# New operation costs, and explicit waits for carries and paired buffers, in the planner that orders a gated-DeltaNet layer's instructions

## The chip, the core and the metric

The kernel runs on one core of one Trainium2 chip. The metric is the device time of one execution in microseconds (us), from launch to end. The engines are named as in the profile: PE is TensorE (PEld is its weight loads), DVE is VectorE, ACT is ScalarE, POOL is GpSimd, and SP is SyncE, on whose queue all DMAs of this kernel are issued.

## What is computed

One layer over 2048 positions of width 1024, in fp32. RMSNorm, then one input projection to 7,184 columns, which feeds two branches; their outputs are joined and projected back by `w_out`, added to the residual, and a gated per-layer embedding and a last RMSNorm follow.

- Branch A, in 8 groups: `gelu(u) * (W_s LN(gelu(v)) + b) * silu(z)` over blocks of 128 positions.
- Branch B, in 8 heads of 128: a causal convolution of four taps over q, k and v, SiLU, L2-normed q and k, and the chunked delta rule in chunks of 64:

```
A = strict_lower((k*beta) k^T * L);  T = inverse(A + I)
u = T (v*beta);  w = T (k*beta*exp(decay));  qk = (q k^T) * L
per chunk:  v_new = u - w S;  o = q_dec S + qk v_new;  S = a S + k_dec^T v_new
```

## The kernel before

**Tiling.** The positions go in two passes of 1024. A product of fp32 matrices with 512 columns is made of three matmuls in a reduced fp32 format (`mm3`: high x high, high x low, low x high), the operands being split into a high and a low part by ACT (copy) and DVE (subtract). Each pass has four units for the branch A input v (`v_unit`), then for each of the 8 heads three units: `kq_unit` (k and q), `vu_unit` (v of branch B, u of branch A) and `zz_unit` (both gates). A unit is four projections of 24 matmuls of 512 columns, so a head has 288 of them. The output projection (`out_stream`) and the gate part (`gate_stream`) come last.

**Work of a head beside the projections.** `conv` (L573) takes a projection out of PSUM with two ACT copies, runs three multiply-adds on DVE, writes the last three columns to `carry` for the next block of 512 positions, and applies SiLU. `decay` (L671) makes the decay matrix L: two selections on POOL (`asel`, tiles R), two matmuls `pd` on PE, an exponential on ACT, one more selection on POOL. `front` (L699), twice a head, transposes k, splits k and q into high and low (`kqhi`, `kqlo`, in the same two buffers R), multiplies them (`pkq`), and scales the results into AT and QK on DVE; AT is stored to DRAM (`atd`, L761). After the second front, `inverse` (L791) loads A back in another layout (`ain`, L802) and inverts all 16 chunk matrices of the head on POOL: 63 steps of a multiplication (`xtmp`) and a subtraction (`xs`), both by `gtt` at L162. The result goes out to DRAM (`td`, L821) and comes back as `Dt` (L828). `chain` (L831) then walks the 8 blocks of 128 positions, five dependent steps each, PE and DVE or ACT in turn; its matmuls are `pc` and `po`. `finish` normalises the head's output (POOL `sso`), and `mix` does branch A.

**What sets the order.** Each engine runs its instructions in the order in which this Python program emits them, and waits on semaphores for operands and buffers. The order comes from a planner, class `Flow` (L36). It has a clock `t`, which each matmul pushes forward by its assumed cost, and a clock for DVE, ACT and POOL, which each operation pushes forward (`op`, L46). The helpers `mm`, `tr`, `act`, `tt`, `stt`, `ts`, `gtt`, `asel` and the like (L114 to L167) hold these costs in ns. `mm` returns the due time of its result, 170 ns after its assumed end; `op` returns the assumed end plus 110 ns. A projection is the stream (`drive`, L85); between any two of its matmuls, every side task whose due time has come goes on and emits what is next, PE work too. `room` (L55) holds a task until an engine's clock is at most 300 ns ahead; `take` and `give` count buffers. So a result that is due sooner in the plan than on the chip is awaited by PE, in order, with all that stands behind it. Two DMA round trips are in the plan as constants: 2500 and 4500 from the front to the first inversion step, 2600 and 4500 from the last step to the chain.

Of the kernel before, what the change touches and what calls it, by code (L numbers as in the profile page):

```python
# [15 lines left out]
F32R = mybir.dt.float32r  # L16
# [14 lines left out]
class Flow:  # L31
# [11 lines left out]
        self.count = 0  # L43
        self.used = {}

    def op(self, eng, cost, after=None):  # L46
        start = max(self.clk[eng], self.t if after is None else after)
        self.clk[eng] = start + cost
        return start + cost + 110.0

    def spawn(self, gen, delay=0.0, prio=0):
        self.tasks.append([prio, self.count, self.t + delay, gen])
# [1 line left out]

    def room(self, eng, slack=300.0):  # L55
        while self.clk[eng] > self.t + slack:
            yield self.clk[eng] - slack

    def free(self, tag):
        return lambda: self.used.get(tag, 0) < CAPS[tag]  # L60

    def take(self, tag):
        while self.used.get(tag, 0) >= CAPS[tag]:
            yield self.t + 150.0
        self.used[tag] = self.used.get(tag, 0) + 1

    def give(self, tag):
        self.used[tag] -= 1
# [32 lines left out]
def trunk(tc, a, out):  # L101
# [7 lines left out]
    fl = Flow()  # L109
# [4 lines left out]
    def mm(o, lhsT, rhs, start, stop):  # L114
        nc.tensor.matmul(o, lhsT, rhs, start=start, stop=stop)  # L115
        n = width(rhs)
        fl.t += max(107.0, 0.4216 * n) if lhsT.dtype == F32R else max(231.0, 1.68 * n)
        return fl.t + 170

    def tr(o, i, ident):  # L120
        nc.tensor.transpose(o, i, ident)
        fl.t += 109.0
        return fl.t + 170

    def act(o, i, func, after=None, **kw):
        nc.scalar.activation(o, i, func, **kw)  # L126
        c = 150 + 0.68 * width(i) + (90 if "accum_out" in kw else 0) + (60 if "scale" in kw else 0)
        t = TABLES.get(func)
        if t and t != fl.table:
            fl.table = t  # L130
            c += 1283
        return fl.op("act", c, after)

    def tt(o, x, y, op, after=None):
        nc.vector.tensor_tensor(o, x, y, op)  # L135
        return fl.op("dve", 69 + 1.04 * width(o), after)

    def stt(o, x, sc, y, op0, op1, after=None):
        nc.vector.scalar_tensor_tensor(o, x, sc, y, op0, op1)  # L139
        return fl.op("dve", 130 + 1.04 * width(o), after)  # L140

    def ts(o, x, s1, s2, op0, op1=None, after=None):
        if op1 is None:
            nc.vector.tensor_scalar(o, x, s1, s2, op0)
        else:
            nc.vector.tensor_scalar(o, x, s1, s2, op0, op1)  # L146
        return fl.op("dve", 70 + 1.0 * width(o), after)

    def vcopy(o, x, after=None):
        nc.vector.tensor_copy(o, x)  # L150
        return fl.op("dve", 65 + 1.04 * width(o), after)

    def recip(o, x, after=None):
        nc.vector.reciprocal(o, x)
        return fl.op("dve", 70 + 6.3 * width(o), after)

    def power(o, x, y, after=None):
        nc.gpsimd.tensor_tensor(o, x, y, ALU.pow)  # L158
        return fl.op("pool", 150 + 190 * width(o), after)

    def gtt(o, x, y, op, after=None):
        nc.gpsimd.tensor_tensor(o, x, y, op)  # L162
        return fl.op("pool", 250 + 1.88 * width(o), after)

    def asel(o, x, after=None):
        nc.gpsimd.affine_select(o, x, [[0, 4], [1, P]], ALU.is_ge, 0.0, 0, -1)  # L166
        return fl.op("pool", 570, after)  # L167

    with ExitStack() as outer:
        outer.enter_context(tc.manual_schedule())  # L170
# [399 lines left out]
            fl.give("uz")  # L570
            gz.append(us[b])

        def conv(ps, f, dest, ready):  # L573
            yield from fl.take("pre")
            yield from fl.take("acc")
            yield from fl.room("act")
            pre = gt("pre", "pre", [P, 515], 2)
            acc = gt("acc", "acc", [P, 512], 3)
            act(pre[:, 3:515], ps, AF.Copy)
            vcopy(pre[:, 0:3], carry[:, f, :])  # L580
            yield fl.clk["act"] - 300
            t = act(acc, ps, AF.Copy, scale=cw[:, f, 3:4])
            fl.give("pj")
            yield t
            for j in (2, 1, 0):
                yield from fl.room("dve")
                t = stt(acc, pre[:, j:j + 512], cw[:, f, j:j + 1], acc, ALU.mult, ALU.add)
            vcopy(carry[:, f, :], pre[:, 512:515])
            fl.give("pre")
            yield t  # L590
            yield from fl.room("act")
            if dest is None:
                t = act(acc, acc, AF.Silu)
            else:
                t = act(dest, acc.rearrange("p (u t) -> p u t", u=4), AF.Silu)
                fl.give("acc")
            yield t
            ready.append(acc)
# [8 lines left out]
        def vu_unit(X, p, ui, h, st):  # L607
            fetch(ui + 1)
            for b in range(2):
                ps = yield from proj(X, ui, 0, b)  # L610
                fl.spawn(conv(ps, 16 + h, None, st["V"]), 170, 1)
                if b == 0:
                    next_w(ui + 1, 0)
            yield lambda: len(mixed) == p * NH + h
            for b in range(2):
                ps = yield from proj(X, ui, 1, b, rest_w(ui + 1) if b == 1 else None)
                fl.spawn(u_post(ps, st["U"]), 170, 1)
# [29 lines left out]
        def kq_unit(X, p, ui, h, st):  # L647
            fetch(ui + 1)
            for b in range(2 if h else 0):
                fl.spawn(decay(p, h, b, st["i"]), 0, 2)  # L650
            for b in range(2):
                yield fl.free("kq")
                fl.used["kq"] = fl.used.get("kq", 0) + 1
                kq = gt("kq", "kq", [P, 4, 2, P], 4)
                ps = yield from proj(X, ui, 0, b)
                fl.spawn(conv(ps, 8 + h, kq[:, :, 0, :], st["C"][b]), 170, 1)
                ps = yield from proj(X, ui, 1, b, rest_w(ui + 1) if b == 1 else None)
                fl.spawn(conv(ps, h, kq[:, :, 1, :], st["C"][b]), 170, 1)
                st["KQ"].append(kq)
                fl.spawn(front(p, h, b, st), 3000, 1)  # L660
                if b == 0:
                    next_w(ui + 1, 0)
# [8 lines left out]
        def decay(p, h, b, i):  # L671
# [3 lines left out]
            while len(fronts) < i + b - 1 or len(Ls) < i + b:  # L675
                yield fl.t + 300
            R = []
            for gg in (gh, gl):
                yield from fl.take("R")
                yield from fl.room("pool", 800)  # L680
                r = gt("R", "R", [P, 4, P], 2, F32R)
                f = asel(r, gg[:, cs, None].bitcast(F32).to_broadcast([P, 4, P]))
                R.append(r)
# [15 lines left out]
        def front(p, h, b, st):  # L699
# [29 lines left out]
            for u2 in range(2):  # L729
                while len(st["C"][b]) < 2:  # L730
                    yield fl.t + 300
                yield from fl.take("R")
                yield from fl.take("R")
                hi = gt("R", "kqhi", [P, 2, 2, P], 2, F32R)
                lo = gt("R", "kqlo", [P, 2, 2, P], 2, F32R)
                yield from split_to(hi, lo, kq[:, u2 * 2:u2 * 2 + 2])
# [495 lines left out]

        done, fronts, inverted, SC, mixed, stored, vdone, prepped, Ls = [[] for _ in range(9)]
        xready = [0, 0]
        xs0 = x_load(0)
        ones = cp.tile([P, P], F32, name="ones")
        nc.vector.memset(ones, 1.0)
# [109 lines left out]
```

## Time and profile before

| | |
|---|---|
| median of 3 runs | 2353.34 us (2353.13 to 2359.31) |
| the profiled execution, its own time | 2353.73 us |
| its span, first to last instruction | 2352.0 us, 34,693 instructions |
| mean granted TensorE clock | 0.987 of 2.4 GHz |
| PE busy | 2269.4 us (96%) |
| DVE, ACT, POOL busy | 1312.9, 1013.6, 1113.1 us |
| ACT table loads | 116 of 1.283 us |

Times in the rows are us from the start of the span, or durations. A matmul's busy time overlaps that of the next: 512 columns are recorded with about 0.40 us, while the next starts about 0.23 us later. So PE's busy share is no measure of how much of its time is work; the distance from start to start is.

### The profile page before, as it was taken

How to read it: one execution, taken by the hardware profiler on the slowest of the kernel's cores; microseconds unless marked ns; L12 is line 12 of the kernel's file. 1: busy time of each engine (PE TensorE's matmuls, PEld its weight loads, DVE VectorE, ACT ScalarE, POOL GpSimd, SP SyncE). 2: the span in 40 equal slices, each digit the busy share in tenths (PEclk: the TensorE clock that was granted, in tenths of full speed). 3: DMA queues.
4: the chain of work that ended last, by engine and by line, in shares of the span. 5: the costliest groups of instructions: out<-in, count | busy, mean ns of one | idle time of the engine just before them, and what ended most of it. 6: DMA issues, size and time to landing. Idle time of an engine off the chain costs nothing.

```text
span 2352.0 us, 34693 instructions
## 1 busy us (share of the span) xinstructions
PE 2269.4 (96%) x11884; PEld 1877.0 (80%) x11884; DVE 1312.9 (56%) x2845; ACT 1013.6 (43%) x2410; POOL 1113.1 (47%) x2246
## 2 busy tenths in 40 slices
PE   9999999999999999999999999999999999999998
PEld 8987777778777779987777777877778878888886
DVE  5465475665655765346556565575564343246665
ACT  5554354444544443444444354444432232244443
POOL 1118668576585682047858668568670000001111
PEclk9999999999999999999999999999999999999999
DMA  5642222323322243222332232223453466452221
GB/s 188 221 128 76 75 87 92 90 80 96 84 84 77 82 159 101 81 81 72 95 92 75 95 89 79 79 80 98 123 164 123 139 201 197 140 190 76 79 79 56
DMA packets 249202, 253.22 MB, mean 108 GB/s; under 512 B 66113, under 2 KB 163905, under 8 KB 249025
## 3 DMA queue, kind: packets, MB, share of 16 engines
q1 hardware_dynamic: 249024, 251.01, 34.1%
q8 instruction: 93, 1.52, 0.3%
q14 instruction: 85, 0.69, 0.1%
HBM read 195.89 MB, written 55.05 MB: 107 GB/s over the span
## 4 chain that ended last, share of the span: by engine, by line
PE 45%; POOL 38%; DMA 7%; issue 5%; DVE 2%; ACT 1%; SPq 1%; POOLq 0%; DVEq 0%; ACTq 0%
POOL xs L162 17%; POOL xtmp L162 16%; PE pso L115 12%; PE pj L115 11%; PE pg L115 7%; PE pv L115 7%; DMA ain<-atd 3%; PE pc L115 2%; PE pe L115 2%; POOL R L166 2%; POOL sso L158 1%; PE pkq L115 1%; DMA Dt<-td 1%; DMA atd<-AT 1%; DMA td<-xs 1%
## 5 line engine op out<-in xcount | busy, mean ns | idle before, releaser
L162 POOL TENSOR_TENSOR xtmp<-ain,xs 128x132 f32<-128x132 f32 (+47 forms) x1008 | 457.7, 454 | 341.0 <-DMA ain<-atd 255.1
L162 POOL TENSOR_TENSOR xs<-xs,xtmp 128x132 f32<-128x132 f32 (+47 forms) x1008 | 470.2, 466 | 79.0
L158 POOL TENSOR_TENSOR rstd<-rstd,nhalf 128x1 f32<-128x1 f32 x64 | 42.9, 677 | 581.5 <-DVE rstd L146 581.5
L115 PE MATMUL pj<-xhi,wlo 128*128 128x512 f32 x768 | 314.8, 410 | 0.0
L115 PE MATMUL pj<-xhi,whi 128*128 128x512 f32 x768 | 314.7, 410 | 0.0
L115 PE MATMUL pj<-xrhi,whi 128*128 128x512 f32 x768 | 314.2, 409 | 0.0
L115 PE MATMUL pj<-xrhi,wlo 128*128 128x512 f32 x768 | 313.6, 408 | 0.0
L115 PE MATMUL pj<-xlo,whi 128*128 128x512 f32 x768 | 312.7, 407 | 0.0
L115 PE MATMUL pj<-xrlo,whi 128*128 128x512 f32 x768 | 312.6, 407 | 0.0
L139 DVE SCALAR_TENSOR_TENSOR acc<-pre,cw,acc 128x512 f32<-128x512 f32 x288 | 228.5, 793 | 31.2 <-ACT acc L126 27.1
L115 PE MATMUL pso<-wohi,ylo 128*128 128x512 f32 x512 | 206.0, 402 | 0.0
L115 PE MATMUL pso<-wolo,yhi 128*128 128x512 f32 x512 | 204.9, 400 | 1.0 <-DVE wolo L135 0.8
L115 PE MATMUL pso<-wohi,yhi 128*128 128x512 f32 x512 | 202.8, 396 | 0.0
L135 DVE TENSOR_TENSOR wlo<-raw,whi 128x512 fp32r<-128x512 f32 x224 | 163.3, 732 | 68.1 <-ACT whi L126 66.6
L126 ACT ACTIVATE yhi<-yraw 128x512 fp32r<-128x512 f32 x128 | 80.2, 629 | 219.8 <-PE pso L115 215.9
L115 PEld LDWEIGHTS pj<-xlo,whi 128*128 128x128 f32 x768 | 146.9, 191 | 25.4
L115 PEld LDWEIGHTS pj<-xhi,wlo 128*128 128x128 f32 x768 | 146.7, 191 | 25.0
L115 PEld LDWEIGHTS pj<-xhi,whi 128*128 128x128 f32 x768 | 147.1, 192 | 24.1
L135 DVE TENSOR_TENSOR ylo<-yraw,yhi 128x512 fp32r<-128x512 f32 x128 | 89.7, 702 | 137.3 <-ACT yhi L126 135.0
L126 ACT ACTIVATE whi<-raw 128x512 fp32r<-128x512 f32 x224 | 140.3, 627 | 60.4 <-PE pj L115 39.7
L115 PEld LDWEIGHTS pj<-xrhi,wlo 128*128 128x128 f32 x768 | 146.4, 191 | 24.9
L115 PEld LDWEIGHTS pj<-xrhi,whi 128*128 128x128 f32 x768 | 146.4, 191 | 23.9
(202 smaller groups left out, 4900.5 us busy)
## 6 DMA issues: line engine op xcount, KB each, us to landing
raw<-in_wu SPq DMA_DIRECT2D x224, 256.0 KB
ain<-atd SPq DMA_DIRECT2D x128, 256.0 KB
yraw<-ysc SPq DMA_DIRECT2D x128, 256.0 KB
vsc<-gv SPq DMA_DIRECT2D x64, 128.0 KB
gn<-vsc SPq DMA_DIRECT2D x32, 256.0 KB
ysc<-gn SPq DMA_DIRECT2D x32, 256.0 KB
ysc<-zb SPq DMA_DIRECT2D x32, 256.0 KB
wo<-in_wo SPq DMA_DIRECT2D x32, 256.0 KB
```

Source lines behind the costliest of these rows:

```text
L115: nc.tensor.matmul(o, lhsT, rhs, start=start, stop=stop)
L126: nc.scalar.activation(o, i, func, **kw)
L135: nc.vector.tensor_tensor(o, x, y, op)
L139: nc.vector.scalar_tensor_tensor(o, x, sc, y, op0, op1)
L158: nc.gpsimd.tensor_tensor(o, x, y, ALU.pow)
L162: nc.gpsimd.tensor_tensor(o, x, y, op)
L166: nc.gpsimd.affine_select(o, x, [[0, 4], [1, P]], ALU.is_ge, 0.0, 0, -1)
```

## The change

The planner gets other numbers. A matmul of 512 columns costs 232 ns in place of 216, one in full fp32 222 in place of 231, and its result is due 220 ns after the end (170 before). Each operation of another engine is due 150 ns after its end (110). The costs of ACT, DVE and POOL operations are written anew; a DVE operation whose inputs are all in SBUF (`local`) costs 1.22 times as much while POOL is busy in the plan. `conv` waits until the block before has written its carry. `take` can ask for two buffers at once, and both users of the R pair do so. No operation, tile, DMA or dependence of the computation is added or removed; only the order in which the engines' instructions are emitted can differ.

```diff
         self.used = {}
-    def op(self, eng, cost, after=None):
+    def op(self, eng, cost, after=None, shared=False):
         start = max(self.clk[eng], self.t if after is None else after)
+        if shared and self.clk["pool"] > start:
+            cost *= 1.22
         self.clk[eng] = start + cost
-        return start + cost + 110.0
+        return start + cost + 150.0
     def spawn(self, gen, delay=0.0, prio=0):
...
     def room(self, eng, slack=300.0):
         while self.clk[eng] > self.t + slack:
-            yield self.clk[eng] - slack
+            yield self.clk[eng] - slack + 1.0
     def free(self, tag):
         return lambda: self.used.get(tag, 0) < CAPS[tag]
-    def take(self, tag):
-        while self.used.get(tag, 0) >= CAPS[tag]:
+    def take(self, tag, n=1):
+        while self.used.get(tag, 0) + n > CAPS[tag]:
             yield self.t + 150.0
-        self.used[tag] = self.used.get(tag, 0) + 1
+        self.used[tag] = self.used.get(tag, 0) + n
     def give(self, tag):
...
     def mm(o, lhsT, rhs, start, stop):
...
         n = width(rhs)
-        fl.t += max(107.0, 0.4216 * n) if lhsT.dtype == F32R else max(231.0, 1.68 * n)
-        return fl.t + 170
+        fl.t += max(109.0, 4 + 0.4453 * n) if lhsT.dtype == F32R else max(222.0, 1.7 * n)
+        return fl.t + 220
     def tr(o, i, ident):
...
         fl.t += 109.0
-        return fl.t + 170
+        return fl.t + 220
+    def local(*aps):
+        return all(x.space == bass.MemoryType.SB for x in aps)
     def act(o, i, func, after=None, **kw):
         nc.scalar.activation(o, i, func, **kw)
-        c = 150 + 0.68 * width(i) + (90 if "accum_out" in kw else 0) + (60 if "scale" in kw else 0)
+        c = 60 + 0.85 * width(i) + (93 if "accum_out" in kw else 0)
+        if local(i):
+            c += 35
+        if not isinstance(kw.get("scale", 1.0), float):
+            c += 100
         t = TABLES.get(func)
...
             fl.table = t
-            c += 1283
+            c += 1290
         return fl.op("act", c, after)
     def tt(o, x, y, op, after=None):
         nc.vector.tensor_tensor(o, x, y, op)
-        return fl.op("dve", 69 + 1.04 * width(o), after)
+        return fl.op("dve", 76 + 1.04 * width(o), after, local(x, y))
     def stt(o, x, sc, y, op0, op1, after=None):
         nc.vector.scalar_tensor_tensor(o, x, sc, y, op0, op1)
-        return fl.op("dve", 130 + 1.04 * width(o), after)
+        return fl.op("dve", (76 if isinstance(sc, float) else 135) + 1.04 * width(o), after, local(x, y))
     def ts(o, x, s1, s2, op0, op1=None, after=None):
...
             nc.vector.tensor_scalar(o, x, s1, s2, op0, op1)
-        return fl.op("dve", 70 + 1.0 * width(o), after)
+        w = width(o)
+        c = 70 + 0.7 * w
+        if not isinstance(s1, float):
+            c = 135 + (2.6 if op1 is not None else 1.04) * w
+        return fl.op("dve", c, after, local(x))
     def vcopy(o, x, after=None):
         nc.vector.tensor_copy(o, x)
-        return fl.op("dve", 65 + 1.04 * width(o), after)
+        return fl.op("dve", 120 + 1.04 * width(o), after, local(x))
     def recip(o, x, after=None):
         nc.vector.reciprocal(o, x)
-        return fl.op("dve", 70 + 6.3 * width(o), after)
+        return fl.op("dve", 185 + 6.3 * width(o), after)
     def power(o, x, y, after=None):
         nc.gpsimd.tensor_tensor(o, x, y, ALU.pow)
-        return fl.op("pool", 150 + 190 * width(o), after)
+        return fl.op("pool", 520 + 165 * width(o), after)
     def gtt(o, x, y, op, after=None):
         nc.gpsimd.tensor_tensor(o, x, y, op)
-        return fl.op("pool", 250 + 1.88 * width(o), after)
+        return fl.op("pool", 330 + 1.6 * width(o), after)
     def asel(o, x, after=None):
         nc.gpsimd.affine_select(o, x, [[0, 4], [1, P]], ALU.is_ge, 0.0, 0, -1)
-        return fl.op("pool", 570, after)
+        return fl.op("pool", 800, after)
     with ExitStack() as outer:
...
             gz.append(us[b])
-        def conv(ps, f, dest, ready):
+        def conv(ps, f, dest, ready, blk):
+            while carried.get(f, 0) < blk:
+                yield fl.t + 150
             yield from fl.take("pre")
...
             vcopy(carry[:, f, :], pre[:, 512:515])
+            carried[f] = blk + 1
             fl.give("pre")
...
                 ps = yield from proj(X, ui, 0, b)
-                fl.spawn(conv(ps, 16 + h, None, st["V"]), 170, 1)
+                fl.spawn(conv(ps, 16 + h, None, st["V"], 2 * p + b), 170, 1)
                 if b == 0:
...
                 ps = yield from proj(X, ui, 0, b)
-                fl.spawn(conv(ps, 8 + h, kq[:, :, 0, :], st["C"][b]), 170, 1)
+                fl.spawn(conv(ps, 8 + h, kq[:, :, 0, :], st["C"][b], 2 * p + b), 170, 1)
                 ps = yield from proj(X, ui, 1, b, rest_w(ui + 1) if b == 1 else None)
-                fl.spawn(conv(ps, h, kq[:, :, 1, :], st["C"][b]), 170, 1)
+                fl.spawn(conv(ps, h, kq[:, :, 1, :], st["C"][b], 2 * p + b), 170, 1)
                 st["KQ"].append(kq)
...
             R = []
+            yield from fl.take("R", 2)
             for gg in (gh, gl):
-                yield from fl.take("R")
                 yield from fl.room("pool", 800)
...
                     yield fl.t + 300
-                yield from fl.take("R")
-                yield from fl.take("R")
+                yield from fl.take("R", 2)
                 hi = gt("R", "kqhi", [P, 2, 2, P], 2, F32R)
...
         xready = [0, 0]
+        carried = {}
         xs0 = x_load(0)
...
```

## Rows read from the trace of the kernel before

**Rows 1.** The page, part 1: busy us (share of the span) and instructions.

```profile
PE 2269.4 (96%) x11884; PEld 1877.0 (80%) x11884; DVE 1312.9 (56%) x2845; ACT 1013.6 (43%) x2410; POOL 1113.1 (47%) x2246
```

**Rows 2.** The chain that ended last, whole span: start, us, what.

```profile
521.23 2.96 DMA td<-xs
...
897.02 3.98 DMA td<-xs
...
1194.16 2.58 DMA td<-xs
...
1757.66 2.81 DMA td<-xs
...
1936.94 160.19 PE pso L115 x688
```

**Rows 3.** The same chain in the stretch 415 to 450 us.

```profile
427.26 2.64 DMA td<-xs
...
430.57 3.12 DMA Dt<-td
...
433.83 0.46 PE pc L115 x2
...
435.68 0.44 PE pvt L121 x4
...
437.50 0.74 PE pkq L115 x6
...
439.36 0.34 DVE QK L135
...
440.04 2.17 DMA atd<-AT
...
442.27 4.17 DMA ain<-atd
...
446.60 0.30 POOL xtmp L162
```

**Rows 4.** The waits of PE: line, releaser: us in total, times, longest.

```profile
PE pd L115 <- POOL R L166: 23.7, 26, 2.8
PE pkq L115 <- DVE kqlo L135: 18.9, 21, 3.6
PE pc L115 <- DMA Dt<-td: 14.2, 9, 3.0
```

**Rows 5.** The waits of SP's DMA queue, the longest.

```profile
SPq L802 <- POOL xs L162: 452.8, 75, 9.7
```

**Rows 6.** Stretch with pass one's heads: PE, PEld, DVE, ACT, POOL busy; clock; DMA.

```profile
165.00:985.00 820.00, 785.85 (x4358) 655.87 (x4358) 474.42 (x1081) 366.66 (x908) 528.94 (x1086) 0.98 0.30 92
```

**Rows 7.** Groups of the page, part 5: busy us, mean ns | idle before, releaser.

```profile
L162 POOL TENSOR_TENSOR xtmp<-ain,xs 128x132 f32<-128x132 f32 (+47 forms) x1008 | 457.7, 454 | 341.0 <-DMA ain<-atd 255.1
L162 POOL TENSOR_TENSOR xs<-xs,xtmp 128x132 f32<-128x132 f32 (+47 forms) x1008 | 470.2, 466 | 79.0
```

**Rows 8.** Instructions on tile R: duration ns min/median/max, first and last start.

```profile
L166 POOL TENSOR_SCALAR_AFFINE_SELECT R<-gh x32: 627/640/1117, 93.5 to 1639.5; 128x512 fp32r<-128x512 f32 x32
L166 POOL TENSOR_SCALAR_AFFINE_SELECT R<-gl x32: 628/635/1086, 94.6 to 1640.1; 128x512 fp32r<-128x512 f32 x32
```

**Rows 9.** Groups by line and shape, columns as in rows 7.

```profile
L139 DVE SCALAR_TENSOR_TENSOR acc<-pre,cw,acc 128x512 f32<-128x512 f32 x288 | 228.5, 793 | 31.2 <-ACT acc L126 27.1
...
L126 ACT ACTIVATE pre<-pj 128x512 f32<-128x512 f32 x96 | 57.4, 598 | 83.3 <-PE pj L115 79.1 <-DVE bn L154 2.0 <-DVE acc L139 1.0
...
L158 POOL TENSOR_TENSOR sso<-sso,nhalf 128x4 f32<-128x4 f32 x32 | 39.8, 1244 | 84.1 <-DVE sso L139 83.6
```

**Rows 10.** POOL's timeline, two steps of one inversion: start us, us, instruction.

```profile
448.85 0.29 POOL L162 TENSOR_TENSOR xtmp<-ain,xs 128x60 f32<-128x60 f32 x1
449.21 0.65 POOL L162 TENSOR_TENSOR xs<-xs,xtmp 128x60 f32<-128x60 f32 x1
```

## The prediction

> **What bounds the kernel now.** I read the page first. PE is busy for 96% of the span, POOL for 47% [rows 1], which looks like a kernel bound by matmuls. That share deceives, so the next view is the chain that ended last, over the whole span. Two things are to be seen in it. In a stretch without a wait, 688 matmuls of 512 columns take 160.19 us, 0.2328 each [rows 2]. And the store `td` of a finished inversion comes once a head: from 427.26 to 897.02 are five heads, from 1194.16 to 1757.66 six, 93.9 us each in both passes [rows 2, 3].
>
> A head has less work for PE than that. 288 projection matmuls at 0.2328 are 67.0 us. The chain's fp32 matmuls, 109 instructions a head at 0.11 (four transposes take 0.44, and these are as short), are 12.0. There are 32 transposes (3.5), 24 `pkq` matmuls (six take 0.74: 2.9), 4 `pd` (0.9) and 8 `pm` (1.8) [rows 2, 3]. Sum 88.1 us. So each head loses 5.8 us, and 16 heads 93. That is the pot.
>
> The third view, the chain in one head, says where it goes [rows 3]. It is a closed loop of 94 us:
>
> - the inversion on POOL from 446.60 to the next `td` at 521.23: 74.6;
> - `td` out, `Dt` in, the first `pc` of the chain (427.26 to 433.83): 6.6;
> - from there to the end of the last scaling of the next head's second front, 439.36 + 0.34: 5.9. PE is in order, and this `pkq` (437.50) stands behind the `pc` that waited for `Dt`;
> - AT out, `ain` in, first inversion step at 446.60: 6.9.
>
> The sum is 94.0, the measured head. POOL is not full, but its inversion lies on a loop that PE's order closes: in the emitted order the chain of head h stands before the last front of head h+1.
>
> The waits of PE show the same loop from PE's side: `pd` on POOL's R 23.7 us, `pkq` on `kqlo` 18.9, `pc` on `Dt` 14.2 [rows 4]. The clock adds to it: granted 0.98 over the heads of pass one [rows 6], 2% of 820 us or 16 us of matmul time lost at 1.2 GHz. All of it is loss inside the loop, not beside it: where PE stalls early in a head, it waits less at `Dt`.
>
> **The change, part by part.**
>
> *POOL's costs.* The two formulas for a step differ by little, but there are 126 in an inversion, with 12,768 columns in all. Old: 126 x 250 + 1.88 x 12,768 = 55.5 us in the plan. New: 126 x 330 + 1.6 x 12,768 = 62.0. Measured: busy 457.7 + 470.2 us over 16 inversions is 58.0, and the gaps between the steps (341.0 - 255.1 - 15.8 + 79.0, over 16) are 9.3: 67.3 [rows 7]. Between them stand four selections R and two for L, 570 each in the old plan, 800 in the new, with a median of 0.64 and up to 1.1 measured [rows 8], and about three `power` of four columns, 910 against 1180, with 1.24 measured [rows 9]. Old 61.7, new 70.3, measured 74.6 as above.
>
> *What the plan loses itself.* It waits for the due time at six loads of `ain` and at L, and goes on only between matmuls. With 110 or 150 ns and half a matmul for each load, and 0.6 for L, I estimate 1.9 us for the old and 2.2 for the new.
>
> *The path as planned*, from the end of the second front to the first `pc`: 7.0 and 7.1 us of constants for the DMA trips, two due-time additions (0.2 and 0.3), the waking between matmuls (0.7) and the inversion. Old: 7.0 + 7.1 + 0.2 + 0.7 + 61.7 + 1.9 = 78.6. New: 87.6. The old plan gives a head 83.5 us of PE (62.2 for projections at 0.216), the new one 88.0. So the old plan puts `pc` 4.9 us ahead of the next front's end, 5.2 in true time; measured are 5.9. The new plan puts it 0.4 us ahead, and the last `pkq` begins 2.2 us ahead of that end (437.50 to 439.70, rows 3). **So `pkq` passes `pc` in PE's order, and the loop opens.** This step carries the forecast.
>
> *What then sets the head.* PE's 88.1, plus what is late next: `Dt`, due after 87.6 in the plan and after 74.6 + 6.6 + 6.9 = 88.1 measured, 0.5 us; plus small waits at the quantum of 0.23 us, which I take as 1 us a head. That is 89.6, 4.3 less than 93.9. Seven heads a pass take part in the loop: 14 x 4.3 = 60. With stalls that short I expect the granted clock to stay at 2.4 GHz through the heads; that is in the 88.1.
>
> *Ends of the passes, first fronts.* Of the pot of 93, the loop holds 14 x 5.8 = 81; 12 belong to the first fronts and the last chains of the passes. The dearer selections and splits reach these as well; I take three quarters, 9, between 0 and 12.
>
> *DVE's costs.* The taps of `conv` cost 662 in the old plan, 667 in the new, 814 while POOL is busy; measured 793 [rows 9]. This keeps `kqlo`, which queues behind taps and splits, from being due early; it is part of the wait at `pkq` above and counts nothing more.
>
> *PE's costs.* A chain step needs as many projection matmuls between as before: for `w`, old 231 + 170 + 198 + 110 = 709, reached with three of 216; new 222 + 220 + 268 + 150 = 860, reached with three of 232. Zero. DMA constants are worth 7% less matmul time; that is in the path above.
>
> *The carry wait.* Two blocks of v follow each other by 24 x 0.2328 = 5.6 us; the first has copied (about 0.6 twice) and done three taps of 0.79 after 3.6 [rows 9], so its carry is written. Zero; if DVE's queue grows by more than 2 us it holds a PSUM bank, and the next projection has 5.6 us more before it needs it.
>
> *The R pair, `room` + 1.* Both users needed two buffers before. Zero, bounded by one selection either way (0.64 to 1.1) [rows 8], covered by the decay being spawned a unit ahead.
>
> *SP's queue.* No DMA is added. The reload of `ain` stands at its head for 452.8 us in 75 waits [rows 5], with the weights behind; a plan nearer to POOL shortens that. PE's longest waits name no weights [rows 4]. So between 0 and, by the row's longest wait, 9.7 us of gain; I take 0, the value that PE's waits speak for.
>
> Sum: 60 + 9 = 69, from the profiled execution's 2353.7 us, which is 0.4 above the median: **2284 us**.
>
> **The rivals.**
>
> *The loop stays closed by a little.* If my plan losses are off by 2 us, `pc` still stands before `pkq`; a head is then 88.1 + 2.2 or more, say 91.5, and the gain 14 x 2.4 = 34: 2320. For it speaks the margin of 1.8 us; against it that 5.2 worked out for the old plan met 5.9. Chance 0.12.
>
> *Collisions eat it.* The same step of 60 columns took 0.29 us and, right after, 0.65 [rows 10]; so a step costs little or much by what DVE does, and the new order packs the same DVE work into shorter heads. Collisions are worth 67.3 - 55.5 = 11.8 us an inversion, if the old formula is that of an undisturbed step (363 for 60 columns; 0.29 and the gap of 0.07 in the rows). If they grow by 2 us, the wait at `Dt` does: 14 x 2 = 28, 2312. Chance 0.10. The Trainium skill (SBUF — State Buffer, "Who interferes with whom") says that a DVE instruction with two SBUF inputs and a GpSimd one that reads SBUF exclude each other, the later one blocked whole; by that rule no formula linear in the columns can be right for a step, and the new plan's mean would miss either way. The two rows agree.
>
> *The order hardly moves.* Both plans shift chain and front alike; 2353. The PE cost rises by 5.4% and the path by 11.5%, so they don't. Chance 0.07.
>
> *Slower: the plan starves its own stream.* `conv` holds one of two projection banks until a `pre` tile is free. If the dearer taps (3 x 0.15 us) and the carry wait hold the bank 1 us too long for each of six projections a head, PE is left without fillers, 96 us over 16 heads against 69: 2380. It decides from 0.72 us each. Against it: a bank has 5.6 us before it is asked for again, a conv needs 3.6 to free its tile, and PE's waits name no bank [rows 4]. Chance 0.12.
>
> **How the numbers follow.** Forecast 0.59, the others 0.12, 0.10, 0.07, 0.12. A measurement of this kernel tells about 0.3%, 7 us, from no change. Faster: 0.59 + 0.12 + 0.10 = 0.81; the same 0.07; slower 0.12. The range reaches down to all of the pot and 10 us of the ends, 2250, and up past the two lesser gains, whose prices may be off by 20, to 2340.
>
> **What would show it.** Right: `td` every 89 to 90 us; the last `pkq` of a head before the first `pc` of the head before, in PE's timeline; waits of `pd` and `pkq` under 10 us together; `Dt` at 10 to 20; clock 1.00 through the heads; POOL's idle time before an inversion down from 16 us to about 12. Wrong: `td` still every 94, or `pc` still ahead of `pkq`; or new waits of PE on ACT's `pre`.

## The result, and the profile after

The changed kernel took 2334.84 us (median of 5 runs, 2331.10 to 2338.44), the kernel before 2359.31 (5 runs beside it): a ratio of 0.9901, interval 0.9878 to 0.9925. That is about 1%, 23 us, where 69 were forecast. The profiled execution took 2334.84 with a span of 2333.1, against 2352.0 before: 18.9 less. Page, part 1, of the kernel after:

```profile
PE 2254.5 (97%) x11884; PEld 1875.8 (80%) x11884; DVE 1306.6 (56%) x2845; ACT 1000.5 (43%) x2401; POOL 1127.6 (48%) x2246
```

Nothing stands out against [rows 1]; the shares tell as little as before. The waits of PE in the kernel after (us in total, times, longest) answer to [rows 4]:

```profile
PE pkq L121 <- DVE kqlo L148: 33.9, 22, 3.4
PE pc L121 <- DMA Dt<-td: 5.6, 5, 2.7
```

`pd` on R has gone (0.5 us left of 23.7) and `Dt` fell from 14.2, but `pkq` went up from 18.9 to 33.9. What stands behind `kqlo` is seen in DVE's timeline in one head of the kernel after (start, us, instruction, in brackets the idle time before it and its releaser):

```profile
705.58 0.25 DVE L159 TENSOR_SCALAR qe<-ss 128x4 f32<-128x4 f32 x1
708.50 0.18 DVE L171 RECIPROCAL bn<-bn 128x4 f32<-128x4 f32 x1 [2.68 <-POOL iv L175]
708.72 0.16 DVE L148 TENSOR_TENSOR bn<-bn,beta 128x4 f32<-128x4 f32 x1
708.80 0.73 DVE L148 TENSOR_TENSOR kqlo<-kq,kqhi 128x512 fp32r<-128x512 f32 x1
```

The reciprocal overwrites `bn`, which POOL's `iv` (the front's `power`) still reads; `iv` stands in POOL's queue among the last steps of the inversion; `kqlo` stands behind the reciprocal in DVE's queue, and PE's `pkq` waits for `kqlo`. So the inversion holds up `kqlo`, although `kqlo` is made of nothing that POOL computes. The chain of waits in the kernel after, at the end of another inversion, answers to [rows 3]:

```profile
801.49 0.21 POOL xs L179
801.70 0.97 POOL iv L175
...
802.70 0.19 DVE bn L171
...
803.07 0.61 DVE kqlo L148
...
803.73 0.88 PE pkq L121 x5
...
804.96 3.15 DMA Dt<-td
...
808.25 0.46 PE pc L121 x2
808.71 0.71 PE pkq L121 x6
...
810.01 0.61 DVE AT L152 x2
...
811.29 2.16 DMA atd<-AT
...
813.53 4.64 DMA ain<-atd
...
818.33 0.30 POOL xtmp L179
```

Here the last `pkq` (808.71) still stands just behind the first `pc` (808.25), and the loop of [rows 3] is whole: `td`, `Dt`, `pc`, `pkq`, AT, `ain`, next inversion, 16.6 us after the end of the last one. In the head before this one the last `pkq` came 4.4 us ahead of `pc`, and the next inversion began 13.3 us after the last.

To see all heads at once, some quantities of each run are set side by side, worked out from the starts and ends of POOL's operations and PE's matmuls. The first three are the inversion (first `xtmp` to last `xs`), the gap to the next inversion and their sum (means of heads 2 to 7 of both passes). "Waits" is POOL's idle time inside an inversion ahead of `sso` and of L, operations that stand between the steps in its queue. The last two give the start of a head's last group of `pkq` against that of the first `pc` of the head before (median of 14; negative is ahead).

```
                     inversion   gap    sum   waits   pkq against pc   ahead in
before                  75.0     19.4   94.4    0.1        +3.4         2 of 14
after                   78.8     14.7   93.5    2.7        -3.8        10 of 14
E4 pool costs           85.4     10.8   96.2    8.0        -8.2        14 of 14
E5 all but pool         74.5     23.1   97.6    0.4        +7.1         0 of 14
E6 dearer steps         85.8     11.5   97.3    8.4        -7.6        14 of 14
E24 L, R on DVE         75.1     19.5   94.6    1.5        +2.6         3 of 14
E8 skip, after          75.6     14.3   89.8    8.5        -3.8        10 of 14
E19 skip, before        70.1     19.6   89.7    3.8        +3.3         2 of 14
```

**The gap fell by 4.7 us, and the inversion grew by 3.8.** The ledger of the span: first to eighth inversion of pass one 657.7 to 649.3, of pass two 654.1 to 649.9, between the passes 204.6 to 198.2, the rest equal within 0.4. So 12.6 us came from the heads and 6.4 from the ends.

What the inversion gained is in POOL's waits and groups. The waits of POOL in the kernel after:

```profile
POOL xtmp L179 <- DMA ain<-atd: 156.1, 11, 18.7
POOL sso L175 <- DVE sso L152: 98.1, 16, 28.3
...
POOL L L183 <- ACT L L135: 42.7, 12, 11.8
```

The page's groups of the steps, as in [rows 7]:

```profile
L179 POOL TENSOR_TENSOR xtmp<-ain,xs 128x132 f32<-128x132 f32 (+47 forms) x1008 | 463.4, 460 | 296.1 <-DMA ain<-atd 156.1
L179 POOL TENSOR_TENSOR xs<-xs,xtmp 128x132 f32<-128x132 f32 (+47 forms) x1008 | 486.8, 483 | 79.0
```

Before, POOL waited 83.6 us for `sso` and 20.1 for L. Inside the 12 inversions the idle time ahead of `sso` went from 0.11 to 1.75 us each, ahead of L from 0.02 to 0.90, and the steps with their small gaps from 66.7 to 68.4; that is 1.6 + 0.9 + 1.7, and 0.4 less for other operations. One such wait, in POOL's timeline of the kernel after:

```profile
1125.16 1.01 POOL L175 TENSOR_TENSOR sso<-sso,nhalf 128x4 f32<-128x4 f32 x1 [6.77 <-DVE sso L152]
1151.78 0.64 POOL L183 TENSOR_SCALAR_AFFINE_SELECT L<-L 128x512 f32<-128x512 f32 x1 [0.91 <-ACT L L135]
```

`sso` is the end of the chain of the head before. Here it stands in POOL's queue some 20 us into the inversion, and all later steps stand behind it. In the kernel before POOL all but waited for it as well; two lines of one inversion, from the timelines of DVE and POOL before:

```profile
453.10 0.27 DVE L139 SCALAR_TENSOR_TENSOR sso<-sso,qe 128x4 f32<-128x4 f32 x1 [0.47 <-ACT junkc L126]
453.44 1.01 POOL L158 TENSOR_TENSOR sso<-sso,nhalf 128x4 f32<-128x4 f32 x1
```

In all seven heads of pass one DVE ended its part of the first `sso` within 0.4 us of the moment at which POOL was ready for it, while L was ready over 2 us before POOL was.

### The profile page after: what moved, and what is told of

Same layout as the page of the kernel before. It is cut to its first block, busy times and chain, and to the rows that moved or that the text cites. A ratio compares the mean times of both kernels' runs of the same rounds, so it can differ in the third digit from the quotient of the medians.

```text
span 2333.1 us, 34673 instructions
## 1 busy us (share of the span) xinstructions
PE 2254.5 (97%) x11884; PEld 1875.8 (80%) x11884; DVE 1306.6 (56%) x2845; ACT 1000.5 (43%) x2401; POOL 1127.6 (48%) x2246
## 4 chain that ended last, share of the span: by engine, by line
PE 61%; POOL 28%; issue 4%; DMA 4%; DVE 2%; ACT 1%; SPq 0%; POOLq 0%; DVEq 0%; ACTq 0%
PE pj L121 20%; PE pso L121 14%; POOL xs L179 12%; POOL xtmp L179 12%; PE pg L121 7%; PE pv L121 6%; PE pc L121 5%; PE po L121 2%; PE pe L121 2%; PE pkq L121 1%; POOL iv L175 1%; POOL R L183 1%; POOL L L183 1%; POOL sso L175 1%; DMA Dt<-td 1%
## 5 line engine op out<-in xcount | busy, mean ns | idle before, releaser
L179 POOL TENSOR_TENSOR xtmp<-ain,xs 128x132 f32<-128x132 f32 (+47 forms) x1008 | 463.4, 460 | 296.1 <-DMA ain<-atd 156.1
L179 POOL TENSOR_TENSOR xs<-xs,xtmp 128x132 f32<-128x132 f32 (+47 forms) x1008 | 486.8, 483 | 79.0
L121 PEld LDWEIGHTS pj<-xrlo,whi 128*128 128x128 f32 x768 | 146.5, 191 | 24.4
```

## The experiments

Theories: A, the `iv`, reciprocal, `kqlo` link is what closes the loop again; B, taking one wait out moves it to another; C, POOL's turn (steps, in-order waits and turn-round) sets the head in either order. The other letters are explained in the expectations that use them.

### E1, E2: the reciprocal no longer waits for POOL

```diff
-            bn = gt("bn", "bn", [P, 4], 4)
+            b8 = gt("bn", "bn", [P, 8], 4)
+            b0, bn = b8[:, 0:4], b8[:, 4:8]
...
-            f = ts(bn, ss[:, 0:4], EPS, None, ALU.add)
-            fiv = power(iv, bn, phalf[:, :4], after=f)
+            f = ts(b0, ss[:, 0:4], EPS, None, ALU.add)
+            fiv = power(iv, b0, phalf[:, :4], after=f)
...
-            recip(bn, bn)
+            recip(bn, b0)
```

E1 is the kernel after with this edit, every engine's order kept.

> The changed kernel with the reciprocal of bn written to other columns than POOL's power reads, so that DVE no longer waits for POOL there; every engine's order stays as it is. Theory A (POOL's backlog reaches PE through this wait: power iv at the end of the inversion's queue, reciprocal bn behind it on DVE, then kqlo, then pkq): pkq's wait falls from 34 to under 8 us, a head from 91.5 to about 89, 35 us less than the changed kernel, about 2300. Theory B (the wait is only where the backlog shows, and Dt takes it over): pkq's wait falls all the same, Dt's rises from 6 to over 25, and the time stays within 8 us of the changed kernel's 2335.

Measured: 2331.03 us, ratio to before 0.9893 (0.9868 to 0.9917), not to be told from the kernel after. PE's largest wait in E1:

```profile
PE pc L121 <- DMA Dt<-td: 41.3, 15, 4.6
```

`pkq`'s 33.9 us are gone, and `Dt` has 41.3 in place of 5.6. The turn-round is in the issues of SP's queue in E1, in the head shown above:

```profile
713.73 0.38 SPq L841 DMA_DIRECT2D td<-xs  x1
716.37 1.22 SPq L848 DMA_DIRECT2D Dt<-td  x2
717.67 1.26 SPq L781 DMA_DIRECT2D atd<-AT  x2
718.99 0.60 SPq L815 DMA_DIRECT2D xs<-in_xinit  x1
720.54 1.27 SPq L822 DMA_DIRECT2D ain<-atd  x2
```

AT now waits behind `Dt`, which waits for `td` to land; the first step starts at 725.0, 11.3 us after the last. E2 is the kernel before with the same edit.

> The kernel before with the same edit. Theory A: in the order of before the head is set by the loop through Dt and pc, so time saved at pkq is mostly waited for again at Dt: 0 to 10 us faster, 2343 to 2353. Rival (each wait is paid by itself): pkq's 19 us and more are saved, about 2330.

Measured: 2358.50, ratio 1.0011 (0.9998 to 1.0025); `pkq`'s wait gone, `Dt` from 14.2 to 38.4 us. The link is real, and alone it is worth nothing in either order: B.

### E3, E4, E5: the parts of the change

E3 is the kernel before with the explicit waits alone (`carried`, the pairs, `room` + 1).

> The kernel before with the explicit waits alone (carry, pair of R, room plus 1) and all costs old. As predicted: no cost and no gain, within 7 us of the kernel before. Rival (taking the pair at once moves decay and front against each other): over 10 us either way.

Measured: 2354.30 (10 runs), ratio 0.9990 (0.9981 to 0.9999): nothing, as expected. E4 adds POOL's three new costs:

```diff
-        return fl.op("pool", 150 + 190 * width(o), after)
+        return fl.op("pool", 520 + 165 * width(o), after)
-        return fl.op("pool", 250 + 1.88 * width(o), after)
+        return fl.op("pool", 330 + 1.6 * width(o), after)
-        return fl.op("pool", 570, after)
+        return fl.op("pool", 800, after)
```

> The kernel before with the explicit waits and the new costs of POOL's operations alone; PE, ACT and DVE costs and the due times stay old. Theory A (what matters is how POOL's planned path stands to PE's planned head): with PE planned at 83.5 us a head and POOL's path at 87, the chain goes behind the next front and POOL is planned as slow as it is; better than the whole change, 2290 to 2315. Rival (the PE costs and due times bring the gain): no better than 2345.

Measured: 2370.64, ratio 1.0061 (1.0035 to 1.0087): slower, against A. The last `pkq` now stands 8.2 us ahead of `pc` in all 14 heads, the gap is down to 10.8, and the inversion up to 85.4; 5.3 us of idle time ahead of `sso` and 2.7 ahead of L are most of that growth of 10.4. POOL's waits in E4, and two in one inversion in its timeline:

```profile
POOL sso L158 <- DVE sso L139: 162.0, 22, 29.6
...
POOL L L166 <- ACT L L126: 51.6, 16, 8.1
```

```profile
663.23 1.01 POOL L158 TENSOR_TENSOR sso<-sso,nhalf 128x4 f32<-128x4 f32 x1 [5.74 <-DVE sso L139]
...
683.08 1.19 POOL L166 TENSOR_SCALAR_AFFINE_SELECT L<-L 128x512 f32<-128x512 f32 x1 [3.32 <-ACT L L126]
```

E5 is the kernel after with POOL's three old costs.

> The changed kernel with the old costs of POOL's operations. Theory A: POOL's path is planned 9 us shorter than a head of PE, the chain stands further ahead of the next front than before, and a head takes about 97 us: slower than before, 2370 to 2400. Rival (PE, DVE and ACT costs and due times bring the gain): 2335 or less.

Measured: 2411.99, ratio 1.0239 (1.0218 to 1.0260): slower, and by more than expected; `pkq` stands behind `pc` in all heads, by 7.1 us in the median; the gap is 23.1, and the waits inside an inversion are down to 0.4. So the change is two shifts of opposite sign. POOL's costs move `pkq` by -11.6 us against `pc` (+3.4 to -8.2), the rest by +3.7 (+3.4 to +7.1); together -7.9 if they add, measured -7.2. Each alone is slower than before; only their sum falls near the middle.

### E6, E13, E14: the steps planned at their measured cost

E6 is the kernel after with `gtt` planned at 360 + 1.75 per column, about the mean measured step.

> The changed kernel with an inversion step planned at 360 + 1.75 a column, 67.7 us an inversion as the kernel before measured, in place of 62.0. If the plan's shortage on POOL is what is left: waits at pkq and Dt under 15 us together, a head of 89 to 90, 2295 to 2310. Theory C (POOL's turn is the bound and no plan shortens it): the waits only change places, 2325 to 2345.

Measured: 2379.43, ratio 1.0091 (1.0071 to 1.0111): slower, and outside both ranges. It is E4's picture (inversion 85.8, gap 11.5), and a new wait: DVE 87.2 us in all on the load of `ws`, against 8.8 in the kernel after, for a memset of a corner of `ws` in `zz_unit` that stands in DVE's queue. E13 moves that memset to `mix`:

```diff
+            nc.vector.memset(ws[64:128, 0:64], 0.0)
...
-            nc.vector.memset(ws[64:128, 0:64], 0.0)
```

> The kernel with an inversion step planned at 360 + 1.75 a column (E6, 2379 us), with one DVE instruction moved: the memset of a corner of ws stands where branch A's mixing first uses ws, no longer right behind the issue of its load. The plan doesn't know the memset, so all else keeps its place. Theory E (what made E6 slow is that memset: DVE waits in order for a small load that SP issues behind td, the reload of xs and ain, 87 us in 13 waits, and PE's chain with it): DVE's wait on ws is gone, the waits of pc on r and vn fall from 43 to under 15 us, 2300 to 2330. Theory C alone (POOL's turn is held up by the longer plan itself): no better than 2365.

Measured: 2347.56, ratio 0.9948 (0.9929 to 0.9967): 32 us below E6, so the memset was most of E6's loss, but still above the kernel after and between the ranges of E and C; `Dt` 25.0 and `pkq` 11.7 us of PE's waits, inversions of 83.2. E14 adds E1's edit.

> E13 with the reciprocal of bn in columns of its own, so that DVE waits for POOL neither there. Theory E: with POOL planned as slow as it is and both in-order waits of DVE gone, PE's 88 us and small waits are left of a head: 2285 to 2310, below E13 by 10 to 25. Rival (Dt takes the wait over, as in E1): within 8 us of E13.

Measured: 2342.20, ratio 0.9927 (0.9906 to 0.9948): within 8 us of E13, as the rival said. A truer cost of the step did not make a better plan here.

### E9, E15, E16: the other waits of the turn-round

E9 issues the stores of AT on ACT's queue (kernel after, `nc.scalar.dma_start` in place of `dma` at L780).

> The changed kernel with the stores of AT issued on ACT's queue in place of SP's; every other instruction keeps its place. Theory C: where these stores stand behind the loads of Dt, which wait for td to land, the turn gets up to 3 us shorter, and the time falls by 10 to 35 us, to 2300 to 2325. Rival (SP's order costs nothing, or ACT pays for the issues): within 8 us of 2335, or slower.

Measured: 2336.79, ratio 0.9921 (0.9898 to 0.9943): no effect, against C. E15 is the kernel after with the memset moved as in E13.

> The changed kernel with that memset moved alone. In it DVE waited for ws 8.8 us in 4 waits: 0 to 9 us less than 2335 by theory E; by theory C 0.

Measured: 2334.38, ratio 0.9889 (0.9869 to 0.9909): none either. E16 makes all three edits (memset, reciprocal, AT on ACT) at once.

> The changed kernel with the memset moved, the reciprocal in columns of its own, and the stores of AT on ACT's queue. In E1, without the wait at pkq, POOL's turn-round of 11.3 us (td, then Dt and AT one behind the other on SP, then xs and ain) closed the head at 91.5 to 92. Theory C: with AT off that queue the turn-round is about 8.5 us, and the head falls by 2 to 3 us, the time from E1's 2331 to 2290 to 2305. Rival: as E1 within 8 us.

Measured: 2345.39, ratio 0.9936 (0.9912 to 0.9960): a miss, 14 us above E1 (10 by the ratios to before). `Dt` takes 49.5 us of PE's time, inversions are 80.9, gaps 13.8. Three links cut, and the sum of inversion and gap is 94.7.

### E8, E19: fewer steps, in both orders

Both leave out 9 of the 63 steps of each inversion (about 9 us of POOL's time a head), so part of the computation is missing; the planner still counts them, so that the order of every engine stays. E8 is made from the kernel after:

```diff
+                if j % 7 == 3:
+                    fl.op("pool", 330 + 1.6 * (kk * n))
+                    f = fl.op("pool", 330 + 1.6 * (kk * n))
+                else:
...
```

> The changed kernel without 9 of the 63 inversion steps (the output isn't the reference's); their planned costs stay, so every other instruction keeps its place. It takes about 10 us of POOL time from a head. Theory C (a head of the changed kernel is one turn of POOL: the inversion of 78 us, waits inside it included, and some 13.5 us from its end to the next first step, through td, Dt, atd and ain on SP's queue): the head falls from 91.5 to what PE needs, about 89, and the time by 30 to 40 us, to 2295 to 2305. Rival D (PE's own small waits set the head): it stays within 8 us of 2335.

Measured: 2279.57, ratio 0.9674 (0.9657 to 0.9690): 55 us below the kernel after, more than expected. PE's largest waits in E8:

```profile
PE pc L121 <- DVE S L152: 3.6, 1, 3.6
...
PE pkq L121 <- DVE kqlo L148: 2.1, 6, 0.6
```

That left open whether the kernel before is held by POOL as well, or by `pkq` behind `pc`. E19 is the same in the kernel before, with its costs.

> The kernel before with 9 of the 63 inversion steps of each head left out (part of the computation is missing), their planned costs kept, so that every engine's order is that of before. Theory C (POOL's turn, and not the order, sets the head in both kernels): 9 to 10 us come off a turn of 94, which leaves PE's 88 to 89 a head as the limit: 2283 to 2305 us, a fall of 50 to 75, and pd's and pkq's waits of rows 4 (23.7 and 18.9 us) fall under 8 each. Rival D (the order of before itself holds the loop, since pkq stands behind pc): the loop shortens by less than half of what was taken out: 2320 us or more, and pd and pkq still wait over 10 us each.

Measured: 2269.56, ratio 0.9625 (0.9601 to 0.9649): 87 us below before, beyond C's range, and 10 below E8. `pkq` still stands behind `pc` (+3.3 us), and yet PE hardly waits in E19:

```profile
PE pkq L115 <- DVE kqlo L135: 3.9, 12, 0.7
...
PE pc L115 <- DMA Dt<-td: 2.4, 3, 1.1
...
PE pd L115 <- POOL R L166: 0.5, 2, 0.3
```

The closed loop is still there and now 70.1 + 19.6 = 89.7 us long, which PE's own work covers: from the second inversion to the eighth a head takes 89.4 us in pass one and 89.9 in pass two, with 0.2 to 1.4 us in which PE has nothing to do. (The first interval of a pass, 79.1 and 80.8 us, has hardly any chain in it.) With 9 us less of POOL's work both orders end at PE's 89 to 90, and the old one is no worse than the new.

So in both orders the head hangs on POOL's work. This does not show that the order counts for nothing: what is left out shortens the loop that PE's order closes as well as POOL's own turn, and E5, with all 63 steps, lost 56 us against before by its order alone.

### E20 to E24: the whole computation, with less on POOL

E20 (kernel after), E21 (kernel before) issue the last 15 of 63 steps on DVE, E22 (kernel after) the last 23:

```diff
...
+                op = tt if j >= 48 else gtt
-                gtt(t_, ains[jc][:, jj, None, j + 1:].to_broadcast([P, kk, n]),
+                op(t_, ains[jc][:, jj, None, j + 1:].to_broadcast([P, kk, n]),
...
-                f = gtt(xs[:, :kk, j + 1:], xs[:, :kk, j + 1:], t_, ALU.subtract)
+                f = op(xs[:, :kk, j + 1:], xs[:, :kk, j + 1:], t_, ALU.subtract)
```

> The kernel after with the last 15 of 63 inversion steps (30 small operations, 14.3 to 16.5 us of POOL's time a head in the trace of after) issued on DVE, planned at DVE's costs; the whole computation. Theory C: POOL's turn falls by 12 us or so, DVE takes on 4 to 6 us a head (of a DVE that is 56% busy), the head is bound by PE: 2275 to 2300 us. Rival F (the steps stand in DVE's in-order queue, wait there for POOL, and hold up the first-step chain): 2320 us or more, with waits of PE's pc on DVE grown by 20 us or more.

> The kernel before with the same last 15 steps on DVE, planned at the costs of before. Theory C: the order matters little once POOL's turn is short: 2280 to 2310 us, within 15 us of E20. Rival D (the durations in the planner are worth 20 us or more of themselves, whatever POOL does): 20 us or more above E20.

> The kernel after with the last 23 of 63 inversion steps on DVE (24 to 26 us of POOL's time a head). Theory C: PE is the floor, so nothing more than E20 comes of it: within 8 us of E20, either way. Rival G (POOL still sets the head in E20): 15 us or more below E20.

Measured: 2383.05 (ratio 1.0110, 1.0086 to 1.0133), 2408.95 (1.0215, 1.0195 to 1.0236) and 2496.54 (1.0591, 1.0573 to 1.0610). All are slower, the more so the more was moved. C's ranges were missed in all three, and rival G's gain in E22 did not come. DVE's timeline in E20:

```profile
706.95 0.33 DVE L167 COPY carry<-pre 128x3 f32<-128x3 f32 x1
708.66 0.27 DVE L148 TENSOR_TENSOR xtmp<-ain,xs 128x105 f32<-128x105 f32 x1 [1.38 <-POOL xs L179]
708.97 0.27 DVE L148 TENSOR_TENSOR xs<-xs,xtmp 128x105 f32<-128x105 f32 x1
...
716.07 0.17 DVE L148 TENSOR_TENSOR xs<-xs,xtmp 128x8 f32<-128x8 f32 x1
```

The 30 operations take 7.6 us of DVE (POOL needs about 15 for them in the kernel after), and DVE stands idle 1.4 us before. For 9 us no tap, `kqlo` or AT goes through DVE; the planner, with them in DVE's clock, puts the front 9 us behind `pc` (E20: +8.9, gap 33.1 with DVE's steps in it). Rival F's hold is there, but not where it was looked for: PE's `pc` waits for DVE 15.5 us in all, 8 more than in the kernel after and not 20, while `kqlo` and AT come late. Between E20 and E21, 26 us show that the order does count once the front is late: rival D's bound of 20 is met.

E23 (kernel after) makes the mask of L on DVE; E24 the four masks R too. The operation is this, one for each `asel`:

```diff
...
+        keep = mgt_r[:, None, :].bitcast(F32).to_broadcast([P, 4, P])
+        nc.vector.scalar_tensor_tensor(o, keep, 0.0, x, ALU.is_equal, ALU.mult)
```

> The kernel after with the mask of L (2 operations of 0.77 to 0.8 us a head, and POOL's waits in its queue for ACT's L, 42.7 us in the trace of after, 3.0 a head) made on DVE, one operation of about 0.75 us each; the whole computation. Theory C: POOL's turn of 91.5 us falls by 1.6 to 4.6, PE needs 88 to 89: 2285 to 2315 us. Rival H (POOL's waits only move to sso, or DVE's queue holds L): within 8 us of after.

> The same, and the 4 masks R a head (about 0.82 us each) made on DVE too, so that 4.9 us of operations and the waits for L leave POOL's turn. Theory C: the floor of PE, 2275 to 2305 us, and at or below E23. Rival F (6 operations more a head, some 4.5 us, fill DVE's in-order queue in front of kqlo and r): 10 us or more above E23.

Measured: 2333.92, ratio 0.9918 (0.9899 to 0.9937), and 2345.81, ratio 0.9965 (0.9951 to 0.9980). POOL's waits for L are gone in E23, those for `sso` are 115.0 in place of 98.1, and the gap is 16.5 in place of 14.7: rival H, nothing gained. In E24 the inversion is back to 75.1, with nearly 5 us less of POOL's own work in it, but the steps with their small gaps have grown to 70.3 us, and the new plan puts `pkq` behind `pc` again in 11 of 14 heads. The chain of waits in E24 is that of [rows 3]:

```profile
709.00 2.65 DMA td<-xs
...
712.30 2.98 DMA Dt<-td
715.33 0.49 PE pc L121 x2
...
718.13 0.71 PE pkq L121 x6
...
720.36 0.26 DVE AT L152
...
721.30 2.15 DMA atd<-AT
723.50 4.51 DMA ain<-atd
728.18 0.82 POOL xtmp L179
```

No version with the whole computation is clearly faster than the kernel after; E1, E15 and E23 are level with it. Theory C is thus right in E8 and E19 as to the direction, and no more than that: wherever the computation was whole, work or waits taken from POOL came back in another place, and the gains that C forecast did not come. No run takes `sso` out of POOL's queue.

## Why the prediction was wrong, step by step

- **The pot and PE's work a head: right to about 1 us.** 88.1 were added up from rows; in E19, free of large waits, the full heads take 89.4 and 89.9, with at most 1.4 us of idle time of PE in one.
- **"So `pkq` passes `pc` in PE's order": mostly right.** It does in 10 of 14 heads, in 2 before. The plan was read to bring `pc` 4.5 us closer to the front, 9.0 by POOL's longer path and 4.5 back by PE's longer head; measured are 7.2, and 11.6 and 3.7 for the two groups of costs (E4, E5).
- **"and the loop opens": right for the gap.** A head of 89.6 with an inversion of 74.6 leaves a gap of 15.0; measured are 14.7. Where `pkq` is ahead of `pc` the gap is 11.8 to 14.0 us, once 16.2; in the four other heads it is 15.6 to 19.6.
- **"What then sets the head": this step failed**, the term 14 x 4.3 = 60 us, which measured 8.4 + 4.2 = 12.6. It kept POOL's inversion at the 74.6 that it had in the old order; it measured 78.8. So 4.2 us a head came back of the 4.3 that were forecast. `sso` and L, operations of POOL's queue that wait for PE's chain and PE's `pd`, began to wait inside the inversion (1.6 and 0.9 us more), and the steps grew dearer by 1.7. [Rows 3] showed the loop that ended last; a second one, over `sso`, was only just short of it, as the two lines of the kernel before show. PE works off the front and the chain one after the other: what the front wins the chain loses, and the chain's end comes back to POOL as `sso`. E4, E6 and E5 show the exchange at its two ends: front ahead by 8.2 and 7.6 us, gap 10.8 and 11.5, inversion 85.4 and 85.8; front behind by 7.1, gap 23.1, inversion 74.5. The waits and times are measured; that the chain's place in PE's order is what makes `sso` late is read from these runs together, since no run changes `sso` alone.
- **POOL "is not full" was the misreading behind it.** 47% of the span hides that in a head POOL has 75 us of inversion and a turn-round whose mean was never below 10.8 us in a run that left all steps on POOL: 86 of 89 us, an estimate from before, E4 and E19. So POOL had next to no room for waits in its queue, and an inversion that grows by 3.8 us eats most of a gap that shrinks by 4.7.
- **Ends of the passes**: 9 us forecast, 6.4 measured. **The carry wait, the R pair, `room`**: zero forecast; E3, 0.999.
- **DVE's and PE's costs** were taken as nothing beyond the path. E5 against E3 shows that the costs other than POOL's move the front by 3.7 us the other way, about the 4.5 that the path had for PE's; they are what keeps the change from E4's loss.
- **SP's queue**: forecast 0. Its longest wait, [rows 5], fell from 452.8 to 277.1 us in all; what that is worth by itself no run shows. Moving AT's stores off the queue (E9) brought nothing.
- **What would show it**: `td` every 89 to 90 us: 93.5 from inversion to inversion. `pd` and `pkq` under 10 us together: 34.4. `Dt` at 10 to 20: 5.6. POOL's idle time before an inversion at about 12 us: 13.1. The granted clock was to be 1.00 and is 0.99 in pass one (0.98 before [rows 6]), 0.98 in pass two.
- **The rivals.** "Collisions eat it" was partly true: the steps grew by 1.7 us an inversion of the 2 it wanted, but in-order waits of 2.5 stand beside them. Two steps of one size still cost two prices in POOL's timeline of the kernel after:

```profile
700.15 0.67 POOL L179 TENSOR_TENSOR xtmp<-ain,xs 128x77 f32<-128x77 f32 x1
700.89 0.33 POOL L179 TENSOR_TENSOR xs<-xs,xtmp 128x77 f32<-128x77 f32 x1
```

  DVE ran two taps of `conv` from 699.00 to 700.63, each with two inputs in SBUF (`acc<-pre,cw,acc`); the step of 0.67 us overlaps them, the one of 0.33 comes after. So the rule of the Trainium skill that was set against [rows 10] (SBUF — State Buffer, "Who interferes with whom") fits this trace as well. "The loop stays closed by a little", at 2320, came nearest in time and not in cause: in most heads the order is the one wanted, and the time is lost inside the inversion. "The order hardly moves" is refuted by the 7.2 us; and of "the plan starves its own stream" the kernel, which got faster, shows nothing.

## What to carry to other kernels

A list schedule on in-order queues ties each engine to the others at several places. Opening the loop that ends last wins only up to the next one. So look for the waits that are just short of zero and sum the whole turn of every engine in the loop, turn-round included, before giving a reorder a price. A cheap test is to take some work out of the suspected engine while its order is kept: E19 told within one run that the old order reaches PE's limit once POOL has 9 us less to do. Costs in such a planner act through differences (`pkq` against `pc`), so one group of costs set anew by itself can be slower than all of them old, as in E4 and E5.

## What the runs showed of the hardware

The granted clock followed the stalls. The stretches with the heads, in E19 (us, PE, PEld, DVE, ACT, POOL busy, clock, DMA share, GB/s):

```profile
165.00:985.00 820.00, 813.27 (x4581) 684.32 (x4580) 497.79 (x1154) 390.61 (x971) 473.52 (x945) 1.00 0.32 96
985.00:1620.00 635.00, 630.81 (x3311) 514.38 (x3310) 396.86 (x893) 306.54 (x775) 428.13 (x854) 1.00 0.31 93
```

With no large wait left the granted clock is 1.00, the level of 2.4 GHz, in both passes, where it was 0.98 in pass one before [rows 6]; in E22, the slowest run, it is 0.962 over the whole execution. So a stall seems to be paid twice, once as a wait and once in the clock after it. This is a likely reason, argued and not shown by itself, why E8 and E19 fell by more than was expected of them.
